# Computing the first four chunks of a squared-relu projection whole, and starting the half-size products with the fifth

## The chip, the cores and the metric

The kernel runs on one core of a Trainium2 chip. The metric is device time in microseconds (us), the median of several executions. Five engines work side by side and meet through semaphores: TensorE (PE; its weight loads are listed as PEld), VectorE (DVE), ScalarE (ACT), GpSimd (POOL) and SyncE (SP, which here only issues DMAs).

## The reference, cut to what matters

Two transformer-like blocks follow one another over 512 positions and 1024 channels, each with two layers, all in float32. The change touches the last part of each layer of the second block:

```python
h = rms_norm(x, g_ffn[l])
x = x + jnp.square(jax.nn.relu(h @ w_ff1[l])) @ w_ff2[l]      # w_ff1: 1024 x 4096
```

Just before it comes `x = x + merged @ w_out[l]`.

## The kernel before, in words

Everything is kept transposed: a tile holds 128 channels by 512 positions. Float32 products are made from rounded parts: a value is split into a high part (ScalarE copies it to the rounded type) and a low part (VectorE subtracts; `split`, lines 126 and 127), and one product is three matmuls, high by high, high by low, low by high (`mm3`, lines 153 to 155). A `gemm` loads one 128-column chunk of weights (512 KB, one DMA), splits it, and runs 8 x 3 = 24 matmuls of 128x512 into one PSUM bank.

The first projection of the squared relu (`w_ff1_2`) has 32 chunks in each layer. The kernel takes them in pairs, 16 `Unit`s, and computes each pair with Strassen's scheme in Winograd's form: the pair is a 2x2 block product (two chunks by two halves of the channels by two halves of the positions), done with seven products of half the positions in place of eight. Each of the seven products is 4 x 3 = 12 matmuls of 128x256 (`product`, lines 194 to 196), so a unit has 84 of them; the same pair through `gemm` would be 48 matmuls of 128x512. The scheme needs sums of both operands. Of the weights, GpSimd forms four 128x512 sums per unit (lines 214 to 217), and they, too, are split. Of the moving operand, `moving_parts` forms for each pair of channel tiles two tiles of differences (lines 168 to 171, tiles `d`) and splits both, the second tile of the pair and the first half of the first tile (tiles `hah`, `hal` for that half, `hh`, `hl` for the rest). That is done once per layer, while the eight chunks of the output projection `w_out_2` are computed (loop at line 996): chunk m gives `x[m]` (line 998), then its square for the norm, then the scaled copy `hf` (line 1001); after every second chunk the pair's parts are made. Every unit needs the parts of all four pairs.

The norm's factor is not applied to the operand. It is a vector over positions that commutes with relu, so it is squared and applied after the second projection (line 1049). Its chain: GpSimd and VectorE add up the squares (tiles `sqa`), TensorE sums them over channels (`ss`, line 271), VectorE takes the inverse square root in some 15 tiny operations (lines 277 to 295) and multiplies it into an identity matrix (`dh`, `dl`), and TensorE spreads it over the partitions (`sp`, lines 302 and 303). In the program this stands between the first unit's products 1, 2, 5 (`one`) and its products 6, 3 (`two`). After every fourth unit a quarter of the second projection (`w_ff2_2`) runs, 8 `gemm`s.

The order of instructions on each engine is not the program's. A planner sorts them at build time by the program's order as priority and by its own prices for each instruction: what is ready in its plan goes ahead of what isn't. At run time each engine keeps to that fixed order. Buffers in rotation: 4 raw weight tiles, 4 high and 4 low weight tiles, 2 tiles for the sums of the weights, 32 tiles `hl` for split operands, 8 `work` tiles, PSUM banks in tags of 3 (`mm`), 2 (`t`), 2 (`sc`) and 1 (`o`).

Of the kernel before, what the change touches and what calls it, by code (L numbers as in the profile page):

```python
# [10 lines left out]
F32R = mybir.dt.float32r  # L11
I32 = mybir.dt.int32
AF = mybir.ActivationFunctionType
ALU = mybir.AluOpType
# [4 lines left out]
HS = S // 2  # L19
D = 1024  # L20
KD = D // P
# [37 lines left out]
def two_blocks(ctx: ExitStack, tc: tile.TileContext, g: dict):  # L59
    nc = tc.nc  # L60
    V, A, G, T = nc.vector, nc.scalar, nc.gpsimd, nc.tensor
# [8 lines left out]
    def uniq(n):  # L70
        cnt[0] += 1
        return f"{n}_{cnt[0]}"

    def work(n="w", shape=(P, S), dt=F32):
        return ap_.tile(list(shape), dt, tag="work", name=uniq(n), bufs=WORK)

    def gate(n="g", shape=(P, S), dt=F32):
        return ap_.tile(list(shape), dt, tag="gate", name=uniq(n), bufs=16)

    def hl(n="hl", dt=F32R):  # L80
        return ap_.tile([P, S], dt, tag="hl", name=uniq(n), bufs=32)
# [4 lines left out]
    def mmps(n="mm"):  # L86
        return ps.tile([P, S], F32, tag="mm", name=uniq(n), bufs=3)
# [10 lines left out]
    def ops(n="o"):  # L98
        return ps.tile([P, S], F32, tag="o", name=uniq(n), bufs=1)


    x = [ap_.tile([P, S], F32, tag=f"x{k}", name=f"x{k}", bufs=1) for k in range(KD)]
# [4 lines left out]
    def col(name, l, c):  # L107
        o, w = VCOL[name]
        o += l * w + c
        return vec[:, o : o + 1]  # L110
# [12 lines left out]
    def split(src, hi, lo, scale=None, n=None):  # L123

        if scale is None:
            A.activation(hi, src, AF.Copy)  # L126
            V.tensor_tensor(lo, src, hi.bitcast(F32), op=ALU.subtract)  # L127
        else:
            A.activation(hi, src, AF.Copy, scale=scale)
            V.scalar_tensor_tensor(lo, src, scale, hi.bitcast(F32), op0=ALU.mult, op1=ALU.subtract)  # L130

    def split_tile(src, scale=None, n="h"):
        hi, lo = hl(n + "h"), hl(n + "l")
        split(src, hi, lo, scale)
        return hi, lo

    def weights(dram, kk, m):

        n = kk * m
        raw = wp.tile([P, CH], F32, tag="raw", name=uniq("raw"), bufs=RAW)  # L140
        nc.sync.dma_start(out=raw[:, :n], in_=dram)
        hi = wp.tile([P, CH], F32R, tag="whi", name=uniq("whi"), bufs=WBUF)
        lo = wp.tile([P, CH], F32R, tag="wlo", name=uniq("wlo"), bufs=WBUF)
        split(raw[:, :n], hi[:, :n], lo[:, :n])
        h = hi[:, :n].rearrange("p (k m) -> p k m", k=kk)
        l = lo[:, :n].rearrange("p (k m) -> p k m", k=kk)
        return h, l

    def mm3(out, terms, first=True, last=True):

        n = len(terms)
        for i, ((wh, wl), (xh, xl)) in enumerate(terms):
            T.matmul(out, lhsT=wh, rhs=xh, start=(first and i == 0), stop=False)  # L153
            T.matmul(out, lhsT=wh, rhs=xl, start=False, stop=False)  # L154
            T.matmul(out, lhsT=wl, rhs=xh, start=False, stop=(last and i == n - 1))  # L155

    def gemm(dram, xs, order=None):

        kk = len(xs)
        h, l = weights(dram, kk, P)  # L160
        out = mmps()
        mm3(out, [((h[:, k, :], l[:, k, :]), xs[k]) for k in order or range(kk)])
        return out

    def moving_parts(b1, b2, odd, o):

        d1, d2 = work("d1"), work("d2")
        V.tensor_tensor(d1[:, :HS], b1[:, HS:], b1[:, :HS], op=ALU.subtract)
        V.tensor_tensor(d1[:, HS:], b2[:, HS:], d1[:, :HS], op=ALU.subtract)
        V.tensor_tensor(d2[:, :HS], b2[:, HS:], b1[:, HS:], op=ALU.subtract)  # L170
        V.tensor_tensor(d2[:, HS:], b2[:, :HS], d1[:, HS:], op=ALU.subtract)
        split(b1[:, :HS], odd[0][:, o : o + HS], odd[1][:, o : o + HS])
        out = [tuple(t[:, o : o + HS] for t in odd)]
        for t in (b2, d1, d2):
            pair = split_tile(t, None, "h")
            out += [tuple(p[:, :HS] for p in pair), tuple(p[:, HS:] for p in pair)]
        return dict(zip((1, 2, 3, 5, 6, 7, 4), out))

# [96 lines left out]
    def mean_eps(ss, n):  # L275
        v = small("v")[:, : ss.shape[1]]
        V.tensor_scalar(v, ss, 1.0 / n, EPS, op0=ALU.mult, op1=ALU.add)
        return v

    def rsqrt(v):  # L280

        y, t = small("y")[:, : v.shape[1]], small("t")[:, : v.shape[1]]
        V.tensor_scalar(y.bitcast(I32), v.bitcast(I32), 1, None, op0=ALU.arith_shift_right)
        V.tensor_scalar(y.bitcast(I32), y.bitcast(I32), -1.0, float(0x5F3759DF), op0=ALU.mult, op1=ALU.add)
        for _ in range(3):
            V.tensor_tensor(t, y, y, op=ALU.mult)
            V.scalar_tensor_tensor(t, t, -0.5, v, op0=ALU.mult, op1=ALU.mult)
            V.scalar_tensor_tensor(y, t, 1.5, y, op0=ALU.add, op1=ALU.mult)
        return y
# [142 lines left out]
    def scaled(p, R, n="e", alloc=work):  # L432
        t = alloc(n)
        V.tensor_tensor(t, p, R, op=ALU.mult)  # L434
        return t
# [5 lines left out]
    p = ops("idle")  # L441
# [11 lines left out]
    for j in range(KD + len(FIRST) - 1):  # L453
        for i, c in enumerate(FIRST):
            k = j - i
            if 0 <= k < KD:
                h, lo = first_w[c]
                mm3(first[c], [((h[:, k, :], lo[:, k, :]), xs[k])], k == 0, k == KD - 1)
    ident = const("ident", (P, P))
    sq = SumSq(V)  # L460
# [12 lines left out]
    for c in (CK, CV):  # L473
        first[c] = scps()
        h, lo = weights(g["w_in"][0, c], KD, P)
# [26 lines left out]
    for l in range(DEPTH):  # L502
        def proj(c):
            return first.pop(c) if c in first else gemm(g["w_in"][l, c], xs)
# [72 lines left out]
        for c in range(2):  # L577
            t, r = ts[c], work("cqr")
            rope(t, cos, sin, r, acopy)
            cq.append(queries(r, hl, "cqx"))  # L580
        t = scaled(proj(CK), R, "ck")
# [12 lines left out]
        for c in range(2):  # L594
            v = scaled(proj(AV + c), R, "av")
            t = work("avt")
            A.activation(t, v, AF.Tanh, scale=0.5)
            u = scaled(proj(AU + c), R, "au")
# [134 lines left out]
        sq = SumSq()  # L733
# [3 lines left out]
        for m in range(KD):  # L737
            p = gemm(g["w_out"][l, m], y, (4, 5, 2, 6, 7, 3, 0, 1))
# [30 lines left out]
    o, w = VCOL["lru_lambda_2"]  # L769
# [21 lines left out]
    for l in range(DEPTH):  # L791
# [13 lines left out]
        for c in range(2):  # L805
            t = scaled(proj(5 + c), R, "kl")
# [4 lines left out]
        for c in range(3):  # L811
            t = scaled(proj(2 + c), R, "ql")
# [164 lines left out]
        for m in range(KD):  # L977
            tg = {0: gate_of(0, m, work), 2: gate_of(2, m, work), 1: tg1[m]}
            h, lo = weights(g["w_br"][l, m], 8, P)
            acc = None  # L980
            for i, k0, ops_ in ((0, 0, ypool), (2, 6, ylru), (1, 2, yo)):
                p = mmps("br")
                mm3(p, [((h[:, k0 + k, :], lo[:, k0 + k, :]), ops_[k]) for k in range(len(ops_))])
                t = work("mgt")
# [7 lines left out]
            mg.append((hi, lo))  # L992

        sq = SumSq()
        hs, halves, odd = [], [], None
        for m in range(KD):
            p = gemm(g["w_out_2"][l, m], mg)
            V.scalar_tensor_tensor(x[m], p, 0.5, x[m], op0=ALU.mult, op1=ALU.add)
            sq.add(x[m])
            t = work("hf")  # L1000
            A.activation(t, x[m], AF.Copy, scale=col("g_ffn_2", l, m))
            halves.append(t)
            if m % 2:
                if m % 4 == 1:
                    odd = hl("hah"), hl("hal")
                hs.append(moving_parts(halves[m - 1], t, odd, m // 2 % 2 * HS))

        sums = sq
        sq = SumSq()
        nxs = []  # L1010
        last = l == DEPTH - 1
        units = [Unit(g["w_ff1_2"][l, 2 * u], g["w_ff1_2"][l, 2 * u + 1], hs) for u in range(16)]

        def relu2(t, n):
# [6 lines left out]
            split(t, hi, lo)  # L1021
            return hi, lo

        f = {}
        for u in range(17):
            if u < 16:
                units[u].one()
            if u == 0:
                rf = rsqrt(mean_eps(token_sums(sums.parts()), D))
                V.tensor_tensor(rf, rf, rf, op=ALU.mult)  # L1030
                Rf2 = spread(rf)
            if u:
                units[u - 1].three()
            if u < 16:
                units[u].two()
            if u:
                units[u - 1].four()
                f[2 * u - 1] = relu2(units[u - 1].bottom, 1)
            if u % 4 or not u:
                f[2 * u] = relu2(units[u].top, 0)  # L1040
                continue
            qt = u // 4 - 1
            fq = [f[8 * qt + c] for c in range(8)]
            if last and qt == 3:
                break
            for m in range(KD):
                p = gemm(g["w_ff2_2"][l, qt, m], fq)
                t = work("ff")
                V.tensor_tensor(t, p, Rf2, op=ALU.mult)  # L1049
                V.tensor_tensor(x[m], x[m], t, op=ALU.add)  # L1050
                if qt == 3:
                    sq.add(x[m])
                    nxs.append(split_tile(x[m], col("g_mix_2", l + 1, m), "x"))
            if u < 16:
                f[2 * u] = relu2(units[u].top, 0)
# [7 lines left out]
    for h in range(2):  # L1063
        t = ap_.tile([P, S + 64], F32, tag="pad", name=uniq("gf"), bufs=3)[:, :S]
# [4 lines left out]
    for h in range(2):  # L1069
# [5 lines left out]
        for b in range(4):  # L1075
# [6 lines left out]
            p = mmps("last")  # L1082
            mm3(p, [((fq[k][0][:, ts], fq[k][1][:, ts]), ws[k]) for k in range(KD)])
            if h == 0 and b % 2 == 0:
                pair = ap_.tile([P, 10 * P], F32, tag="prob", name=uniq("yh"), bufs=PROBS)
            yh = pair[:, S * (b % 2) : S * (b % 2) + S] if h == 0 else xt
            V.scalar_tensor_tensor(yh, p, rf[:, b : b + 1], xt, op0=ALU.mult, op1=ALU.add)
            sq = work("sq")
# [122 lines left out]
```

## Time and profile before

| | |
|---|---|
| median of 3 runs | 1929.95 us (1928.28 to 1930.03) |
| profiled execution, its own time | 1930.22 us |
| its span, first to last instruction | 1928.3 us, mean granted TensorE clock 0.992 |
| PE busy | 1872.7 us (97%), 10028 matmuls |
| DVE busy | 1376.5 us (71%) |
| ACT busy | 933.0 us (48%) |
| POOL busy | 274.9 us (14%) |

Matmuls overlap in the pipeline, so the duration of one is longer than the distance from one start to the next; what a matmul costs is read from that distance. "Idle before" is the time that an engine stood still before an instruction, and the arrow names what it then waited for.

### The profile page before, as it was taken

What the parts mean: (1) busy time and instruction counts of PE and PEld (TensorE: products, weight loads), DVE (VectorE), ACT (ScalarE), POOL (GpSimd) and SP (SyncE); (2) the same over time, 40 slices, a digit from 0 to 9 for tenths busy, and PEclk for the clock granted to TensorE, in tenths of its full rate; (3) what the DMA queues carried; (4) which work ended last, traced back from release to release, by engine and by line L of the source; (5) the groups of instructions that cost most, each with busy time, mean ns of one, the idle gap of its engine ahead of it and who ended that gap; (6) DMA issues with size and microseconds to landing.
All of it is one profiled execution on the core that took longest, in us unless ns stands there. A gap on an engine that the chain in (4) does not pass through costs nothing.

```text
span 1928.3 us, 26111 instructions
## 1 busy us (share of the span) xinstructions
PE 1872.7 (97%) x10028; PEld 1565.1 (81%) x10028; DVE 1376.5 (71%) x2304; ACT 933.0 (48%) x1567; POOL 274.9 (14%) x211
## 2 busy tenths in 40 slices
PE   9999999999989999998999999999999989999998
PEld 7877878878857788878898998777788879889896
DVE  8997669976788545588576777687455687667584
ACT  7565445654358533265253444367433455344362
POOL 0000100002100000043133141000000132424121
PEclk9999999999989999999999999999999999999999
DMA  6322323222212223221322323222232313232321
GB/s 216 107 80 82 98 88 96 77 77 90 64 44 95 71 87 98 99 88 66 109 99 88 110 88 120 62 85 87 66 98 92 105 44 113 88 107 94 125 88 44
DMA packets 53693, 175.41 MB, mean 91 GB/s; under 512 B 6208, under 2 KB 10176, under 8 KB 53568
## 3 DMA queue, kind: packets, MB, share of 16 engines
q1 hardware_dynamic: 53568, 173.74, 27.8%
q8 instruction: 79, 1.29, 0.3%
q14 instruction: 46, 0.38, 0.1%
HBM read 171.62 MB, written 2.10 MB: 90 GB/s over the span
## 4 chain that ended last, share of the span: by engine, by line
PE 79%; DVE 12%; issue 4%; ACT 4%; DVEq 0%; ACTq 0%
PE mm L154 17%; PE mm L153 17%; PE mm L155 17%; DVE ul L127 2%; PE o L417 2%; PE ua L194 2%; PE t L337 2%; PE ua L196 2%; PE ua L195 2%; PE sc L860 2%; PE br L153 2%; PE br L154 2%; PE br L155 2%; DVE fl L127 1%; PE sc L553 1%
## 5 line engine op out<-in xcount | busy, mean ns | idle before, releaser
L126 ACT ACTIVATE whi<-raw 128x1024 fp32r<-128x1024 f32 (+2 forms) x250 | 252.1, 1012 | 529.4 <-PE mm L154 388.6
L153 PE MATMUL mm<-xh,whi 128*128 128x512 f32 x904 | 361.7, 401 | 0.4 <-DVE ql L434 0.4
L155 PE MATMUL mm<-xh,wlo 128*128 128x512 f32 x904 | 357.6, 396 | 0.0
L154 PE MATMUL mm<-xl,whi 128*128 128x512 f32 x904 | 356.8, 395 | 0.0
L127 DVE TENSOR_TENSOR wlo<-raw,whi 128x1024 fp32r<-128x1024 f32 (+2 forms) x250 | 300.6, 1205 | 36.6 <-ACT whi L126 35.0
L153 PEld LDWEIGHTS mm<-xh,whi 128*128 128x128 f32 x904 | 170.5, 189 | 37.7 <-issue 3.8
L155 PEld LDWEIGHTS mm<-xh,wlo 128*128 128x128 f32 x904 | 170.4, 189 | 36.5 <-issue 2.2
L154 PEld LDWEIGHTS mm<-xl,whi 128*128 128x128 f32 x904 | 170.6, 189 | 35.3 <-issue 2.7
L153 PE MATMUL mm<-fh,whi 128*128 128x512 f32 x448 | 174.4, 389 | 0.0
L154 PE MATMUL mm<-fl,whi 128*128 128x512 f32 x448 | 174.4, 389 | 0.0
L155 PE MATMUL mm<-fh,wlo 128*128 128x512 f32 x448 | 174.3, 389 | 0.0
L214 POOL TENSOR_TENSOR s<-raw 128x512 f32<-128x512 f32 x32 | 48.3, 1510 | 833.9 <-DVE hl L127 461.3
L1049 DVE TENSOR_TENSOR ff<-mm,rstd 128x512 f32<-128x512 f32 x56 | 38.7, 691 | 119.8 <-PE mm L155 119.6
L434 DVE TENSOR_TENSOR lg<-mm,rstd 128x512 f32<-128x512 f32 x48 | 33.2, 691 | 119.6 <-PE mm L155 119.5
L194 PE MATMUL ua<-hh,uh 128*128 128x256 f32 x384 | 110.5, 288 | 6.6 <-DVE bottom L248 5.7
L195 PE MATMUL ua<-hl,uh 128*128 128x256 f32 x384 | 109.1, 284 | 0.0
L196 PE MATMUL ua<-hh,ul 128*128 128x256 f32 x384 | 109.0, 284 | 0.0
L155 PEld LDWEIGHTS mm<-fh,wlo 128*128 128x128 f32 x448 | 84.1, 188 | 17.6
L153 PEld LDWEIGHTS mm<-fh,whi 128*128 128x128 f32 x448 | 84.1, 188 | 17.2
L154 PEld LDWEIGHTS mm<-fl,whi 128*128 128x128 f32 x448 | 84.1, 188 | 17.1
L126 ACT ACTIVATE uh<-s 128x1024 fp32r<-128x1024 f32 x64 | 67.5, 1059 | 60.9 <-PE mm L154 26.6
L127 DVE TENSOR_TENSOR ul<-s,uh 128x1024 fp32r<-128x1024 f32 x64 | 87.0, 1377 | 6.0 <-ACT uh L126 6.0
(366 smaller groups left out, 4319.0 us busy)
## 6 DMA issues: line engine op xcount, KB each, us to landing
raw<-in_w_in SPq DMA_DIRECT2D x124, 512.0 KB, 3.5
raw<-in_w_ff SPq DMA_DIRECT2D x120, 512.0 KB, 3.3
raw<-in_w_out SPq DMA_DIRECT2D x32, 512.0 KB, 3.4
raw<-in_w_br SPq DMA_DIRECT2D x16, 512.0 KB, 3.3
raw<-in_w_last SPq DMA_DIRECT2D x8, 512.0 KB, 4.0
raw<-in_w_q SPq DMA_DIRECT2D x12, 192.0 KB, 2.3
x<-in_xT SPq DMA_DIRECT2D x8, 256.0 KB, 5.8
bends<-in_rpb SPq DMA_DIRECT2D x8, 256.0 KB, 4.7
```

Of the source, the lines that this page charges most:

```text
L126: A.activation(hi, src, AF.Copy)
L127: V.tensor_tensor(lo, src, hi.bitcast(F32), op=ALU.subtract)
L153: T.matmul(out, lhsT=wh, rhs=xh, start=(first and i == 0), stop=False)
L154: T.matmul(out, lhsT=wh, rhs=xl, start=False, stop=False)
L155: T.matmul(out, lhsT=wl, rhs=xh, start=False, stop=(last and i == n - 1))
L194: T.matmul(out, lhsT=h[:, ks], rhs=xh, start=(first and j == 0), stop=False, skip_group_check=True)
L195: T.matmul(out, lhsT=h[:, ks], rhs=xl, start=False, stop=False, skip_group_check=True)
L196: T.matmul(out, lhsT=lo[:, ks], rhs=xh, start=False, stop=(last and j == 3), skip_group_check=True)
L214: G.tensor_tensor(s1[:, :S], a21, a22, op=ALU.add)
L337: T.matmul(out, lhsT=in_, rhs=ident, is_transpose=True, start=True, stop=True)
L417: T.matmul(out[64 * j : 64 * j + 64, i * P : (i + 1) * P], lhsT=v(b), rhs=t[:, at[j, e]], start=(b == keys[i][0]), stop=(b == keys[i][1] - 1))
L1049: V.tensor_tensor(t, p, Rf2, op=ALU.mult)
```

## The change

The first two units of each layer are dropped. Their four chunks are computed by `gemm` from whole split tiles, with relu on ScalarE, the square on VectorE, and a split. To have whole tiles, every scaled tile `t` is now split over all 512 positions as soon as it is there (`whole`), and `moving_parts` takes its halves from these splits. The parts of the last pair are made after the first two of the four chunks. The sum of squares comes after the split. The norm's factor now stands behind the first products of the third unit (u = 2), which is the first one left.

```diff
-    def moving_parts(b1, b2, odd, o):
+    def moving_parts(b1, b2, p1, p2):
         d1, d2 = work("d1"), work("d2")
 ...
-        split(b1[:, :HS], odd[0][:, o : o + HS], odd[1][:, o : o + HS])
-        out = [tuple(t[:, o : o + HS] for t in odd)]
-        for t in (b2, d1, d2):
-            pair = split_tile(t, None, "h")
+        out = [tuple(p[:, :HS] for p in p1)]
+        for pair in (p2, split_tile(d1, None, "h"), split_tile(d2, None, "h")):
             out += [tuple(p[:, :HS] for p in pair), tuple(p[:, HS:] for p in pair)]
 ...
         for m in range(KD):
             p = gemm(g["w_out_2"][l, m], mg)
             V.scalar_tensor_tensor(x[m], p, 0.5, x[m], op0=ALU.mult, op1=ALU.add)
-            sq.add(x[m])
             t = work("hf")
             A.activation(t, x[m], AF.Copy, scale=col("g_ffn_2", l, m))
             halves.append(t)
-            if m % 2:
-                if m % 4 == 1:
-                    odd = hl("hah"), hl("hal")
-                hs.append(moving_parts(halves[m - 1], t, odd, m // 2 % 2 * HS))
+            whole.append(split_tile(t, None, "h"))
+            sq.add(x[m])
+            if m % 2 and m < KD - 1:
+                hs.append(moving_parts(halves[m - 1], t, *whole[m - 1 : m + 1]))
 ...
+        f = {}
+
+        def plain(u):
+            for c in (2 * u, 2 * u + 1):
+                p = gemm(g["w_ff1_2"][l, c], [whole[k] for k in (0, 2, 4, 6, 1, 3, 5, 7)])
+                t = work("relu")
+                A.activation(t, p, AF.Relu)
+                V.tensor_tensor(t, t, t, op=ALU.mult)
+                f[c] = gate("fh", dt=F32R), gate("fl", dt=F32R)
+                split(t, *f[c])
+
+        plain(0)
+        hs.append(moving_parts(*halves[KD - 2 :], *whole[KD - 2 :]))
+        plain(1)
 ...
-        for u in range(17):
+        for u in range(2, 17):
             if u < 16:
                 units[u].one()
-            if u == 0:
+            if u == 2:
                 rf = rsqrt(mean_eps(token_sums(sums.parts()), D))
                 V.tensor_tensor(rf, rf, rf, op=ALU.mult)
                 Rf2 = spread(rf)
-            if u:
+            if u > 2:
                 units[u - 1].three()
             if u < 16:
                 units[u].two()
-            if u:
+            if u > 2:
                 units[u - 1].four()
                 f[2 * u - 1] = relu2(units[u - 1].bottom, 1)
-            if u % 4 or not u:
+            if u % 4:
                 f[2 * u] = relu2(units[u].top, 0)
                 continue
```

## Rows read from the trace of the kernel before

**Rows 1.** TensorE's waits, 813 to 1190 us: us in total, times, longest.
```profile
PE sp L302 <- DVE dh L299: 4.1, 1, 4.1
PE ua L194 <- DVE bottom L248: 2.8, 4, 0.8
PE ss L271 <- DVE sqa L333: 1.0, 1, 1.0
PE ub L195 <- DVE hl L127: 0.8, 1, 0.8
```
**Rows 2.** Timeline of TensorE: start us, us, engine, line, operation [idle before, releaser].
```profile
813.46 0.39 PE L153 MATMUL mm<-mh,whi 128*128 128x512 f32 x1
...
856.98 0.28 PE L194 MATMUL ua<-hah,uh 128*128 128x256 f32 x1
...
870.01 1.02 PE L271 MATMUL ss<-ones,sqa 128*128 128x1 f32 x8 [1.04 <-DVE sqa L333]
870.89 0.37 PE L194 MATMUL ua<-hah,uh 128*128 128x256 f32 x1
...
873.37 0.28 PE L196 MATMUL uc<-hh,ul 128*128 128x256 f32 x1
877.75 0.80 PE L302 MATMUL sp<-dh,ones_r 128*128 128x512 f32 x1 [4.10 <-DVE dh L299]
...
881.11 0.28 PE L194 MATMUL ua<-hh,uh 128*128 128x256 f32 x1
...
886.86 0.28 PE L194 MATMUL ua<-hah,uh 128*128 128x256 f32 x1
...
1560.79 0.28 PE L194 MATMUL ua<-hah,uh 128*128 128x256 f32 x1
...
1573.84 1.02 PE L271 MATMUL ss<-ones,sqa 128*128 128x1 f32 x8 [1.04 <-DVE sqa L333]
...
1581.58 0.79 PE L302 MATMUL sp<-dh,ones_r 128*128 128x512 f32 x1 [4.09 <-DVE dh L299]
...
1589.01 0.28 PE L194 MATMUL uc<-hh,uh 128*128 128x256 f32 x1
```
**Rows 3.** Stretches: length, busy time by engine, granted clock, DMA share, GB/s.
```profile
877.75:880.69 2.94, 2.94 (x11) 2.75 (x12) 1.06 (x5) 1.24 (x3) 0.00 (x0) 0.50 0.00 0
1581.58:1587.29 5.71, 5.71 (x24) 5.52 (x25) 1.49 (x6) 3.48 (x6) 0.00 (x0) 0.50 0.00 0
```
**Rows 4.** Timeline of TensorE, the same chain of a norm among full-size matmuls.
```profile
266.06 0.95 PE L271 MATMUL ss<-ones,sqa 128*128 128x1 f32 x8
...
271.65 0.50 PE L302 MATMUL sp<-dh,ones_r 128*128 128x512 f32 x1 [0.17 <-DVE dh L299]
```
**Rows 5.** Timeline of VectorE.
```profile
267.92 1.23 DVE L127 TENSOR_TENSOR wlo<-raw,whi 128x1024 fp32r<-128x1024 f32 x1
...
850.04 1.51 DVE L170 TENSOR_TENSOR d<-hf,hf 128x256 f32<-128x256 f32 x1
...
856.33 0.69 DVE L998 SCALAR_TENSOR_TENSOR x<-mm,x 128x512 f32<-128x512 f32 x1
...
863.41 0.41 DVE L170 TENSOR_TENSOR d<-hf,hf 128x256 f32<-128x256 f32 x1
...
864.09 0.68 DVE L127 TENSOR_TENSOR hl<-hf,hh 128x512 fp32r<-128x512 f32 x1
...
871.99 0.15 DVE L277 TENSOR_SCALAR v<-ss 128x4 f32<-128x4 f32 x1
...
872.38 1.15 DVE L284 TENSOR_SCALAR y<-y 128x4 int32<-128x4 int32 x1
873.56 1.18 DVE L286 TENSOR_TENSOR t<-y 128x4 f32<-128x4 f32 x1
...
875.17 0.16 DVE L286 TENSOR_TENSOR t<-y 128x4 f32<-128x4 f32 x1
```
**Rows 6.** Tile `s` alone, one stretch: DVE, ACT, POOL busy, clock, DMA.
```profile
857.00:878.00 21.00, 4.66 (x3) 2.12 (x2) 8.41 (x6) 0.99 0.15 51
```
**Rows 7.** Timeline of GpSimd.
```profile
872.21 1.29 POOL L216 TENSOR_TENSOR s<-raw,s 128x512 f32<-128x512 f32 x1 [1.23 <-DVE v L277]
873.46 1.26 POOL L217 TENSOR_TENSOR s<-raw,raw 128x512 f32<-128x512 f32 x1
```

More of the change, by code (lines that the diff above doesn't have):

```diff
@@ L994, in two_blocks @@
         sq = SumSq()
-        hs, halves, odd = [], [], None
+        hs, halves, whole = [], [], []
         for m in range(KD):
@@ L1022, in relu2 @@
             return hi, lo
-        f = {}
-        for u in range(17):
+        for u in range(2, 17):
             if u < 16:
                 units[u].one()
-            if u == 0:
+            if u == 2:
                 rf = rsqrt(mean_eps(token_sums(sums.parts()), D))
```

## The prediction

> **What bounds the kernel now.** I read the page first: TensorE is busy for 97% of the span, so a change counts only through what TensorE executes and where it stands still. The view of waits says where it stands still: in the second block's squared relu it waits at the start of each layer, once for long on the spreading of the norm's factor (`sp`, 4.1 us) and several times for under 1.1 us on `sqa`, `hl` and its kin, while all later units together show four waits of at most 0.8 us on `bottom` [rows 1]. Last I read TensorE's timeline, for the distances from start to start.
>
> Full-size matmuls: from 813.46 to 856.98 run the 8 x 24 = 192 of the output projection, 43.52 / 192 = 0.2267 us each. Half-size ones: from 881.11 to 886.86 run four products of 12, 5.75 / 48 = 0.12 us each [rows 2]. So the scheme pays 53% per half-size matmul, and a unit's 84 cost 10.08 us.
>
> What the start of a layer loses: from 856.98 to 870.01 there are 63 half-size matmuls (five products of 12 and three of the next unit), 7.56 us of work in 13.03 us; 5.47 us are lost while the last pair's parts and the sum of squares come late. The second layer has the same 13.05 us from 1560.79 [rows 2]. The parts come late because VectorE is behind: TensorE is done with chunk 6 at 856.98 - 24 x 0.2267 = 851.5, yet `x[6]` is only computed at 856.33, behind the third pair's subtractions, of which one took 1.51 us where the same one takes 0.41 elsewhere [rows 5].
>
> Then the norm: behind `ss` stand 21 half-size matmuls, the last at 873.37, and `sp` starts at 877.75: 877.75 - 873.49 = 4.26 us of standing still [rows 2]. The granted clock behind it is 0.50 (1.2 GHz) for 2.9 us in the first layer and 5.7 us in the second [rows 3]; from `sp` to 881.11 there are 12 half-size matmuls and two full ones, 1.89 us of work in 3.36; in the second layer, from 1581.58 to 1589.01, 36 and two, 4.77 in 7.43 [rows 2]. So the slow clock costs 1.5 and 2.7 us, and the norm's wait with it 2 x 4.26 + 1.5 + 2.7 = 12.7 us in two layers.
>
> **The change part by part.** *More matmul work.* Four units of 10.08 us become four pairs of chunks of 48 x 0.2267 = 10.88 us: 4 x 0.80 = +3.2 us, all on the path, since TensorE has nothing else.
>
> *The waits at the start go.* The first chunk takes its operands in the order 0, 2, 4, 6, 1, 3, 5, 7, so it needs tile 6 after 9 matmuls, 2.0 us in (859.0 on the old time axis), and tile 7 after 21, 4.8 us in (861.7). Chunk 7 of the output projection ends with TensorE at 857.0; then one update (0.69), the scaled copy and high part on ScalarE, the low part (0.68) [rows 5], with the hand-overs some 3.5 us: 860.5, 1.2 us early. Tile 6 has 5.4 us more and can bear most of the lateness that it has now. The last pair's differences, which stand in the way now, come after the first two chunks. The chunks' weights are four DMAs of 512 KB in place of the same four; a raw tile is given back after one split instead of after GpSimd's four sums, so nothing behind them on SP's queue is later. I count 0.3 us per layer as left over (bounds 0, by the 1.2 us of slack, and 5.5, by the loss now): gain 2 x (5.5 - 0.3) = 10.4 us. The wait for `sqa` is in this sum; with 22 us of full-size chunks behind it, it can't come last again.
>
> *Wider splits and other relus.* Tiles 0, 2, 4, 6 are split over 512 instead of 256 positions, the four chunks are squared on VectorE (nearest row 0.68), while eight GpSimd sums a layer and the splits of two units fall away. Cover: TensorE's 21.8 us of whole chunks. VectorE's work in that stretch, unstretched: update 0.69, two weight splits 2.5, the last tile's low part 0.68, the last pair 4 x 0.41 + 2 x 0.68 = 3.0, `sqa` 0.7, four squares and four low parts 5.4, the third unit's weights 4.3, the start of the fourth's 1.9: 19.2 us [rows 5]. It fits, at 88%. If it does not, the third unit is late (the last rival).
>
> *The norm's factor moves* behind the third unit's first three products. What matters is what the planner puts between `ss` and `sp`. Among full-size matmuls the chain took 271.65 - 266.06 = 5.59 us, and the planner had filled it to within 0.17 us [rows 4], which is 4.4 us or some 20 matmuls of 0.2267. Among half-size ones it put 21 [rows 2], which take 2.5 us. It counts a half-size matmul like a full one, so its plan falls short by 5.59 - 0.88 (`ss`) - 2.52 = 2.2 us even with a chain that runs freely. The other 2 us of today's 4.26 are two tiny operations of the chain that took 1.15 and 1.18 us instead of 0.16 [rows 5], at the very times of two GpSimd sums [rows 7]. In the plan TensorE has ready work of higher priority until the third unit's three products are issued, so I expect `ss` right behind them and `sp` behind the 24 matmuls of `two`: half-size ones again. Bounds for the wait: 0.3 (the row among full-size matmuls) and 4.3 (today's). I take the middle of 2.2 and 4.3, since GpSimd is busy beside the units for a part of the time: 3.2 us, and the smaller of the two prices of the slow clock, 1.5: 4.7 per layer, 9.4 in two. Gain 12.7 - 9.4 = 3.3 us.
>
> The collision has a rule. The Trainium skill, GPSIMD Engine Reference, section Specifications, says that GpSimd's SBUF interfaces are shared with VectorE and that they contend with VectorE's instructions of two SBUF inputs or in a two-port mode; the subtraction of 1.51 us against 0.41 agrees. By the rule alone every such operation beside a GpSimd sum is late; what that would make of the whole chunks is the last rival.
>
> *Sum.* 1930.2 (the profiled execution, 1928.3 of span and 1.9 around it) + 3.2 - 10.4 - 3.3 = 1919.7. That execution stands 0.3 us above the median of the runs, so I predict 1919.5.
>
> **The rivals.**
>
> A, the forecast: 1919.5. With a free chain and no slow clock (2 x 2.2 left of 12.7, no rest at the start): 1930.2 + 3.2 - 10.9 - 8.3 = 1914.2. With 1 us left at each start and the norm's wait as it is: 1930.2 + 3.2 - 8.9 = 1924.5. Chance 0.53.
>
> B, the norm's wait goes too: the planner finds a gap earlier and puts `ss` and `sp` among the whole chunks, where its price for a matmul holds. For it: the squares are summed 15 us before the third unit starts, and the row among full-size matmuls. Against it: the order in the program, and no gap in sight. 0.3 us left per layer and no slow clock: 1930.2 + 3.2 - 10.4 - 12.1 = 1910.9. Chance 0.23.
>
> C, the first chunks wait instead: `x[6]` and tile 7 stay behind the third pair's parts on VectorE, as `x[6]` does now by 4.8 us. For it: the splits in front of them are wider. Against it: the third and fourth units' sums start later. Half of the loss comes back (2.7 per layer), the norm's wait stays: 1930.2 + 3.2 - 5.5 = 1927.9, no measurable change. So the change would do what it says and gain nothing. Chance 0.14.
>
> D, slower: VectorE does not get through the whole chunks. GpSimd's sums took 8.4 us in the 21 us after 857 [rows 6]; if the third and fourth units' sums fall into the same stretch and hold up VectorE by all of it, 19.2 + 8.4 = 27.6 us stand against 21.8, the last pair's parts and the third unit's weights, lowest in priority, are 5.8 us late, and the norm's wait stays: 1930.2 + 3.2 - 10.9 + 11.6 = 1934.1. It decides where the last pair's splits end after the fourth chunk. This is the rule of the Trainium skill (GPSIMD Engine Reference, Specifications) taken in full. Against it: in the rows not every operation beside a sum is stretched, and the planner can put parts earlier. Chance 0.10.
>
> **How the numbers follow.** About 0.2% (3.9 us) can be told from no change, so faster means under 1926.1. A gives nearly all of its 0.53, B 0.23, C some 0.03: 0.79. The same: most of C and a little of A, 0.12. Slower: 0.09, from D. The range from 1909 to 1927 takes in B with 2 us to spare and A whole, some 0.8; C and D lie outside. A's own range is 1914 to 1924.5.
>
> **What would show it.** Right: no TensorE wait over 0.5 us in the four whole chunks, whose 96 matmuls take 21.8 us; one wait of 2 to 4.3 us on `dh` per layer, behind some 20 to 24 half-size matmuls, with a clock of 0.50 behind it; units as before from the fourth on. Wrong: `sp` among 128x512 matmuls (B); waits on `hl` inside the first chunk (C); waits on `hl` or `ul` at the third unit's first product (D).

## The result, and the profile after

The changed kernel takes 1919.93 us (median, 1919.07 to 1921.59) against 1929.99 us of the kernel before beside it: ratio 0.9949, 95% interval 0.9932 to 0.9966. That is 10 us or 0.5% faster; 1919.5 was forecast, with a range of 1909 to 1927. The profiled execution took 1920.23 us with a span of 1918.3 us, 10.0 us less than before. The total came out as forecast, and in part by luck: one of its terms was wrong by 4.4 us, and a gain of 3.6 us that was not counted made up for it.

TensorE's waits between 813 and 1190 us, the stretch of [rows 1] (us in total, times, longest):

```profile
PE sp L300 <- DVE dh L297: 3.8, 1, 3.8
PE ua L192 <- DVE bottom L246: 1.5, 2, 0.8
PE ss L269 <- DVE sqa L331: 0.7, 1, 0.7
```

The waits on `hl` and its kin at the start of a layer are gone. The wait on `dh` is as good as unchanged, the one on `sqa` is still there, and of four waits on `bottom` two are left.

TensorE's timeline after, in both layers (start, us, engine, line, operation): first matmul of the output projection, first half-size one, `ss`, `sp`, the first matmul behind the stretch at the slow clock, first one of the second projection (`ss` and `sp` in the first layer only).

```profile
814.20 0.39 PE L153 MATMUL mm<-mh,whi 128*128 128x512 f32 x1
...
879.82 0.28 PE L192 MATMUL ua<-hh,uh 128*128 128x256 f32 x1
...
886.88 1.02 PE L269 MATMUL ss<-ones,sqa 128*128 128x1 f32 x8 [0.68 <-DVE sqa L331]
...
895.67 0.50 PE L300 MATMUL sp<-dh,ones_r 128*128 128x512 f32 x1 [3.83 <-DVE dh L297]
...
902.04 0.28 PE L192 MATMUL uc<-hh,uh 128*128 128x256 f32 x1
...
915.00 0.40 PE L153 MATMUL mm<-fh,whi 128*128 128x512 f32 x1
...
1513.41 0.39 PE L153 MATMUL mm<-mh,whi 128*128 128x512 f32 x1
...
1578.74 0.28 PE L192 MATMUL ua<-hh,uh 128*128 128x256 f32 x1
...
1601.92 0.28 PE L192 MATMUL uc<-hh,uh 128*128 128x256 f32 x1
...
1614.88 0.40 PE L153 MATMUL mm<-fh,whi 128*128 128x512 f32 x1
```

The ends of the same stretch in the kernel before, where its first row is the first of [rows 2]:

```profile
918.88 0.40 PE L153 MATMUL mm<-fh,whi 128*128 128x512 f32 x1
...
1517.27 0.39 PE L153 MATMUL mm<-mh,whi 128*128 128x512 f32 x1
...
1623.93 0.40 PE L153 MATMUL mm<-fh,whi 128*128 128x512 f32 x1
```

From the first matmul of the output projection to the first of the second projection the kernel before takes 918.88 - 813.46 = 105.4 us and 106.7 us, the changed one 100.8 and 101.5: 4.6 and 5.2 us less, 9.8 of the 10.0. The rest differs by less than 1 us in any stretch (0.7 more ahead of the first layer's stretch, 0.95 less behind the second's). With 0.2267 and 0.12 us per matmul, and some 1.35 for `ss` and `sp`, the work in this stretch is 192 full and 396 half-size matmuls before (92.4 us) and 288 and 228 after (94.0). By this count the price of 1.6 us per layer is there as forecast. What is lost to standing still and to the slow clock falls from 13.0 and 14.3 us to 6.8 and 7.5.

| lost, us, both layers | before | after |
|---|---|---|
| start, to the first half-size matmul after the whole chunks (before: to `ss`) | 11.0 | 0.4 |
| the norm: `ss` to the end of the slow clock (after: with the wait on `sqa`) | 12.8 | 13.9 |
| from there to the second projection (two waits on `bottom` per layer, with what stands about them) | 3.6 | 0 |

In the view of waits those on `bottom` of the first quarter, the products ahead of the first part of the second projection, are 0.45 and 0.82 us in each layer; from start to start of the matmuls they cost 1.8.

### The profile page after: what moved, and what is told of

Same layout as the page of the kernel before. It is cut to its first block, busy times and chain, and to the rows that moved or that the text cites. A ratio compares the mean times of both kernels' runs of the same rounds, so it can differ in the third digit from the quotient of the medians.

```text
span 1918.3 us, 25753 instructions
## 1 busy us (share of the span) xinstructions
PE 1872.8 (98%) x9884; PEld 1560.5 (81%) x9884; DVE 1353.7 (71%) x2288; ACT 922.5 (48%) x1543; POOL 248.3 (13%) x195
## 4 chain that ended last, share of the span: by engine, by line
PE 82%; DVE 10%; ACT 4%; issue 4%; DMA 0%; SPq 0%; DVEq 0%; ACTq 0%
PE mm L154 18%; PE mm L153 18%; PE mm L155 18%; PE o L415 2%; PE t L335 2%; DVE ul L127 2%; PE ua L192 2%; PE ua L194 2%; PE ua L193 2%; PE sc L858 2%; PE br L153 2%; PE br L154 2%; PE br L155 2%; PE sc L551 1%; DVE wlo L127 1%
## 5 line engine op out<-in xcount | busy, mean ns | idle before, releaser
L126 ACT ACTIVATE whi<-raw 128x1024 fp32r<-128x1024 f32 (+2 forms) x258 | 260.6, 1014 | 537.5 <-PE mm L154 389.8
L127 DVE TENSOR_TENSOR wlo<-raw,whi 128x1024 fp32r<-128x1024 f32 (+2 forms) x258 | 315.4, 1225 | 39.0 <-ACT whi L126 37.7
L192 PE MATMUL ua<-hh,uh 128*128 128x256 f32 x448 | 128.3, 286 | 3.4 <-DVE bottom L246 3.4
L193 PE MATMUL ua<-hl,uh 128*128 128x256 f32 x448 | 127.6, 285 | 0.0
L194 PE MATMUL ua<-hh,ul 128*128 128x256 f32 x448 | 127.6, 285 | 0.0
L323 POOL TENSOR_TENSOR sqa<-sq,sq 128x512 f32<-128x512 f32 x8 | 12.0, 1503 | 629.7 <-DVE d L170 456.1
L212 POOL TENSOR_TENSOR s<-raw 128x512 f32<-128x512 f32 x28 | 42.5, 1517 | 381.7 <-DMA raw<-in_w_ff 216.9
L192 PEld LDWEIGHTS ua<-hh,uh 128*128 128x128 f32 x448 | 87.0, 194 | 5.1 <-DVE bottom L246 4.8
```

The lines of the kernel that those rows point to most:

```text
L192: T.matmul(out, lhsT=h[:, ks], rhs=xh, start=(first and j == 0), stop=False, skip_group_check=True)
L193: T.matmul(out, lhsT=h[:, ks], rhs=xl, start=False, stop=False, skip_group_check=True)
L194: T.matmul(out, lhsT=lo[:, ks], rhs=xh, start=False, stop=(last and j == 3), skip_group_check=True)
L212: G.tensor_tensor(s1[:, :S], a21, a22, op=ALU.add)
```

## The experiments

Two start from the kernel before (the order of the splits alone, and the second of the two with the later spreading), the others from the changed kernel. Each was timed in turn with the kernel before on the same chip; the medians of the kernel before, 1929.8 to 1930.0 us, agree.

**The norm's chain among the whole chunks.**

```diff
         plain(0)
+        rf = rsqrt(mean_eps(token_sums(sums.parts()), D))
+        V.tensor_tensor(rf, rf, rf, op=ALU.mult)
+        Rf2 = spread(rf)
         hs.append(moving_parts(*halves[KD - 2 :], *whole[KD - 2 :]))
 ...
-            if u == 2:
-                rf = rsqrt(mean_eps(token_sums(sums.parts()), D))
-                V.tensor_tensor(rf, rf, rf, op=ALU.mult)
-                Rf2 = spread(rf)
```

> The chain of the norm's factor is moved up, to between the second and the third whole chunk; 24 full-size matmuls then stand between ss and sp, where 32 half-size ones stood. Theory (the planner counts half-size matmuls as full ones, so the chain is covered only among full ones): the wait on dh falls from 3.8 us to 0.5 or less in each layer, no clock of 0.50 behind it, the wait on sqa goes; of the 13.9 us that the norm costs in two layers some 12.5 go: 1907.5 us. Rival (VectorE is the bound of the whole chunks, 88% full by my count, and the chain's 5 us push the third unit's weights and the last pair's parts late): waits on ul or hl at the third unit of 2 to 3 us per layer, 1913 to 1919 us.

1912.45 us, ratio 0.9912 (0.9898 to 0.9925): 7.5 us below the changed kernel, between the two expectations. `sp` still waits, and VectorE's and GpSimd's timelines of this run show for what:

```profile
872.18 1.25 DVE L281 TENSOR_SCALAR y<-v 128x4 int32<-128x4 int32 x1
873.47 0.17 DVE L282 TENSOR_SCALAR y<-y 128x4 int32<-128x4 int32 x1
873.67 1.13 DVE L284 TENSOR_TENSOR t<-y 128x4 f32<-128x4 f32 x1
```
```profile
871.79 1.61 POOL L212 TENSOR_TENSOR s<-raw 128x512 f32<-128x512 f32 x1 [8.93 <-issue]
873.48 1.30 POOL L213 TENSOR_TENSOR s<-s,raw 128x512 f32<-128x512 f32 x1
```
```profile
PE sp L300 <- DVE dh L297: 2.0, 1, 2.0
```

Two tiny operations take 1.25 and 1.13 us where they take 0.17 and 0.16 alone, 2.05 us too long, beside two of GpSimd's sums; the one between them, which was under way when the second sum began, took 0.17. The wait is 2.0 us. Among full-size matmuls the plan covers the chain, but not what GpSimd adds to it. No unit waits on `ul` or `hl`, so it is not the rival's mechanism: two waits of 2.0 us and the slow clock behind one of them (1.5 us) are about what is missing to 1907.5.

**Only two whole chunks.**

```diff
         hs.append(moving_parts(*halves[KD - 2 :], *whole[KD - 2 :]))
-        plain(1)
 ...
-        for u in range(2, 17):
+        for u in range(1, 17):
```

(and u = 1 in place of u = 2 in the conditions)

> Only the first two chunks of each layer are whole, the half-size products begin with the third chunk. Theory (two chunks are too short a cover for the last pair's parts, and a run of three units brings back the wait on bottom): 1.6 us less of matmul work, 1 us per layer of waits on d or hl at the first unit, 1 us per layer on bottom: 1919.9 - 1.6 + 4 = 1922 us. Rival (the start waits are covered by any whole chunk, and a whole pair costs just its 0.8 us): 1918.3 us.

1927.45 us, ratio 0.9987 (0.9978 to 0.9996): 7.5 us worse than with four chunks, and 5 worse than I expected.

```profile
PE sp L300 <- DVE dh L297: 5.5, 1, 5.5
PE ua L192 <- DVE bottom L246: 2.0, 3, 0.8
PE mm L154 <- DVE hl L127: 1.6, 2, 0.9
```

The wait comes back at the start, but on `hl` inside the whole chunks, not at the first unit; and the one on `dh` grows to 5.5, with a weight split of 2.19 us and three operations of the chain at 1.25, 1.10 and 1.19 us, beside four sums from 879.61 to 885.7. One wait on `bottom` in the first quarter, 0.45 us, is back as well, on the third of its three units. So the start loses 2.4 us per layer (240 full matmuls in 56.84 us) where I had expected 1, and the chain's part, 1.7 us more per layer on `dh`, stood in neither expectation.

**The order of the splits alone, in the kernel before.**

```diff
             V.scalar_tensor_tensor(x[m], p, 0.5, x[m], op0=ALU.mult, op1=ALU.add)
-            sq.add(x[m])
 ...
                 hs.append(moving_parts(halves[m - 1], t, odd, m // 2 % 2 * HS))
+            sq.add(x[m])
```

> The kernel before, with one part of the change alone: the sum of squares comes behind the splits and the differences instead of ahead of them; no chunk is whole. Theory (the start waits come from half-size products that want the last pair at once): within 1 us of before, 1929 to 1930.5 us, with the four waits at the layer's start in place. Rival (the order of the splits made the gain): 1921 to 1925 us, and the four waits shorter by half or more.

1930.92 us, ratio 1.0005 (0.9996 to 1.0014): no change. In the first layer the wait on `sqa` is gone and the two on the last tile (`ub`) fall from 1.5 to 0.2 us, the two on `hah` and `hal` grow, and the wait on `dh` takes the rest back:

```profile
PE sp L302 <- DVE dh L299: 5.3, 1, 5.3
PE ua L194 <- ACT hah L126: 0.9, 1, 0.9
PE ua L195 <- DVE hal L127: 0.9, 1, 0.9
```

At the start 4.7 us are lost per layer in place of 5.5 (54 half-size matmuls in 11.2 us). So the order alone does not give the gain at the start; and what is saved ahead of the norm's chain can be lost in it.

**No sums of GpSimd beside the chain.**

```diff
+            if self.sums:
                 s1 = ap_.tile(...)
 ...
                 G.tensor_tensor(s2[:, S:], a11, a21, op=ALU.subtract)
+            else:
+                s1, s2 = raws
 ...
+        units = [Unit(g["w_ff1_2"][l, 2 * u], g["w_ff1_2"][l, 2 * u + 1], hs, u != 4) for u in range(16)]
```

> The changed kernel with GpSimd's four sums left out for the fifth unit of each layer (u = 4), the one whose sums fall into the norm's chain; the raw weights are split in their place, so the fifth unit's products are not the reference's. TensorE's order stays the same. Theory (collision of GpSimd's sums with VectorE's tiny operations): the chain gets 3.0 us shorter, the wait on dh falls from 3.8 to about 0.9 us, the clock stays at 1.00, and 2 x (3.0 + 1.5 to 2.7) are gained: 1910 us. Rival (the planner's price alone makes the wait): the wait stays at 2.2 us or more, 1915 to 1919 us.

1909.22 us, ratio 0.9895 (0.9881 to 0.9908), 10.7 us below the changed kernel, as the theory had it. VectorE's timeline of the changed kernel, then GpSimd's, then this run's VectorE (its lines stand three further down) and its wait:

```profile
887.95 0.16 DVE L275 TENSOR_SCALAR v<-ss 128x4 f32<-128x4 f32 x1 [1.21 <-PE ss L269]
888.14 1.11 DVE L281 TENSOR_SCALAR y<-v 128x4 int32<-128x4 int32 x1
...
890.89 1.15 DVE L286 SCALAR_TENSOR_TENSOR y<-t,y 128x4 f32<-128x4 f32 x1
892.07 1.19 DVE L284 TENSOR_TENSOR t<-y 128x4 f32<-128x4 f32 x1
```
```profile
887.94 1.29 POOL L213 TENSOR_TENSOR s<-s,raw 128x512 f32<-128x512 f32 x1
890.73 1.29 POOL L214 TENSOR_TENSOR s<-raw,s 128x512 f32<-128x512 f32 x1 [1.50 <-DVE t L284]
891.97 1.26 POOL L215 TENSOR_TENSOR s<-raw,raw 128x512 f32<-128x512 f32 x1
```
```profile
888.42 0.17 DVE L284 TENSOR_SCALAR y<-v 128x4 int32<-128x4 int32 x1
...
890.22 0.16 DVE L289 SCALAR_TENSOR_TENSOR y<-t,y 128x4 f32<-128x4 f32 x1
890.42 0.16 DVE L287 TENSOR_TENSOR t<-y 128x4 f32<-128x4 f32 x1
```
```profile
PE sp L303 <- DVE dh L300: 0.9, 1, 0.9
```

Each of the three operations starts within 0.2 us of a sum and ends where the sum ends. Without the sums they take 0.16 to 0.17, 2.96 us less in all, and the wait falls by 2.94, from 3.83 to 0.89 us. The slow clock goes with it: the granted clock stays at 1.00 behind `sp` in both layers. What is left, 0.9 us, is what the planner's order leaves uncovered. The Trainium skill, GPSIMD Engine Reference, section Specifications, names the contention for SBUF interfaces with VectorE's operations of two SBUF inputs or in a two-port mode. The trace agrees for L286 and L284, which have two inputs, and adds the size: the VectorE operation is held to the end of the sum. L281 has one input and was held as well; in which mode it runs, no run shows.

Not every VectorE operation is held. In the changed kernel, VectorE's timeline and then GpSimd's:

```profile
857.14 1.78 DVE L127 TENSOR_TENSOR hl<-hf,hh 128x512 fp32r<-128x512 f32 x1
858.85 0.68 DVE L996 SCALAR_TENSOR_TENSOR x<-mm,x 128x512 f32<-128x512 f32 x1
```
```profile
856.64 1.74 POOL L213 TENSOR_TENSOR s<-s,raw 128x512 f32<-128x512 f32 x1
858.45 1.62 POOL L214 TENSOR_TENSOR s<-raw,s 128x512 f32<-128x512 f32 x1
```

The split of `hf` is held (0.68 alone, [rows 5]); the update behind it, which reads its product `mm` from PSUM, runs inside a sum at its usual 0.68. In the traces of the ten kernels, around the two layers' squared relu, 61 single operations that read a product from PSUM began inside a GpSimd operation (its last 0.1 us left out), and none took over 0.15 us more than its shortest; of 379 without such an input 370 did.

**The spreading one unit later, and the same in the kernel before.**

```diff
-                Rf2 = spread(rf)
 ...
                 units[u].two()
+            if u == 3:
+                Rf2 = spread(rf)
```

(in the kernel before: `if u == 1`)

> The changed kernel, with only the spreading of the norm's factor moved down by one unit (behind the products 6, 3 of the fourth unit); ss and the inverse square root stay. Between ss and sp stand 83 half-size matmuls (10 us) instead of 32. Theory (the wait is the chain's length less the work put beside it, so enough work beside it removes it and the slow clock behind it): no wait on dh, clock 1.00, 2 x 4.0 + 1.5 + 2.7 us gained: 1907.7 us. Rival (VectorE is late anyway, and the standing still let it catch up): waits on bottom or ul of the later units take back half: 1913 us or more.

1910.96 us, ratio 0.9904 (0.9889 to 0.9919): 9 of the 12.2 us. The chain met three sums here too (1.12, 1.14 and 1.22 us), but under 83 matmuls. Some wait is left, 1.4 us, and for another reason. The factor was there at 892.7 (L292 at 892.69 is the first rounding), but the multiplications into the identity had slid behind the units' splits in VectorE's queue:

```profile
892.69 0.17 DVE L292 CAST yh<-y 128x4 fp32r<-128x4 f32 x1
...
893.91 1.22 DVE L127 TENSOR_TENSOR ul<-raw,uh 128x1024 fp32r<-128x1024 f32 x1
895.05 0.42 DVE L246 TENSOR_TENSOR bottom<-ua,keep 128x256 f32<-128x256 f32 x1
895.38 1.22 DVE L127 TENSOR_TENSOR ul<-s,uh 128x1024 fp32r<-128x1024 f32 x1
896.51 0.87 DVE L297 TENSOR_SCALAR dh<-c_ident,yh 128x128 fp32r<-128x128 f32 x4
```
```profile
PE sp L300 <- DVE dh L297: 1.4, 1, 1.4
```

The rival's place (`bottom`) shows hardly more than in the changed kernel, 3.8 us in both layers against 3.4.

> The kernel before, no chunk whole, with only the spreading moved down by one unit in the same way (72 half-size matmuls between ss and sp instead of 21). Theory (the norm's wait and the waits at the start are separate losses): the start's waits stay (5.5 us per layer), the wait of 4.26 us and the slow clock go: 1929.9 - 2 x 4.26 - 4.2 = 1917.2 us. Rival (as above, half comes back on bottom): 1923 us.

1919.56 us (1919.22 to 1923.79), ratio 0.9954 (0.9941 to 0.9966), between the expectations: one moved line in the kernel before gives as much as the whole change. The profiled execution was the longest, 1923.79 us. In it the waits at the start stay as in [rows 1], as expected; the waits on `dh` are 1.1 us in one layer and 2.6 in the other. Here the multiplication into the identity itself is held beside a sum:

```profile
882.56 1.88 DVE L299 TENSOR_SCALAR dh<-c_ident,yh 128x128 fp32r<-128x128 f32 x4
```

The same four together took 0.87 us in the run above. The slow clock did not go as expected: in the first layer it came between `ss` and `sp`, behind the waits at the start, and in the second behind the 2.6 us. The two waits on `bottom` in the first quarter are gone too, though all four of its units are there.

**Six whole chunks, without and with the later spreading.**

```diff
         plain(1)
+        plain(2)
 ...
-        for u in range(2, 17):
+        for u in range(3, 17):
```

(and u = 3 in place of u = 2; with the later spreading also `if u == 4` behind `two`)

> The changed kernel with six whole chunks instead of four, half-size products from the seventh on. Theory (a further pair costs its 0.8 us and hides nothing more, since the start's waits are gone with four): 1919.9 + 1.6 = 1921.5 us, the wait on dh within 0.5 us of 3.8. Rival (each unit less relieves VectorE, and the norm's chain runs freely): the wait falls below 2 us, 1914 us.

1910.21 us, ratio 0.9899 (0.9886 to 0.9913): 9.7 us below four chunks, where I expected 1.6 above. GpSimd's timeline, the stretch of the chain (length, busy times of PE, PEld, DVE, ACT and POOL, clock, DMA) and TensorE's wait:

```profile
887.92 1.74 POOL L215 TENSOR_TENSOR s<-raw,raw 128x512 f32<-128x512 f32 x1
```
```profile
897.00:901.60 4.60, 3.76 (x32) 3.56 (x30) 4.15 (x21) 0.38 (x1) 0.00 (x0) 1.00 0.00 0
```
```profile
PE sp L300 <- DVE dh L297: 0.9, 1, 0.9
```

The order between `ss` and `sp` is the same 32 half-size matmuls. But GpSimd's last sum ends at 889.7, the chain runs from 896.9 to 901.5 with GpSimd idle (the fifth column of busy times, 0.00), since behind the fifth unit the weights of the second projection come in line before those of the sixth: GpSimd's next sum begins at 932.2. The wait is 0.89 us, to the hundredth the one without sums. The price of a pair is there: by the same count as above the stretch holds 94.8 us of work, and 96.3 are spent.

> Six whole chunks and the spreading one unit later together. Theory: as the four chunks with the later spreading, plus the price of a pair in each layer: 1.6 us above that run, about 1909.3 us. Rival (VectorE's relief counts): the same as that run or below.

1908.29 us, ratio 0.9887 (0.9874 to 0.9901), the fastest version: 11.6 us below the change, and 1.9 us below six chunks alone. No wait is left but the 0.8 us on `bottom` in later quarters:

```profile
PE ua L192 <- DVE bottom L246: 1.6, 2, 0.8
```

It is not slower than four chunks with the later spreading (1910.96), as the price alone would have made it, because those still waited 1.4 us on `dh` and 0.7 on `sqa` per layer: 1.6 - 2.8 - 1.4 = -2.6, measured -2.7.

## Why the prediction was right, point by point

**The price of whole chunks**, +3.2 us: held. The work in the stretch grew by 1.6 us per layer, by the count of its matmuls.

**The waits at the start**, -10.4: held, 11.0 - 0.4 = 10.6 us. With two whole chunks 1.6 us of waits stand there again in the first layer, and the order alone saves nothing in total. Part of the same step failed: the wait on `sqa` was to go for good, and is 0.7 us per layer as it moved. The squares' last addition stood in VectorE's order behind weight splits of the fourth unit, at 886.05 us, some 28 us after the last chunk of the output projection.

**The norm's wait**, -3.3: failed. Forecast were 9.4 us left of 12.7; measured are 13.9 with the wait on `sqa` (0.8 per layer with its hand-over), so some 12.2 without it: nearly nothing gained (per layer 4.0 us of standing still, and 1.6 and 2.6 us of slow clock where I took the smaller price for both). The step had two parts. That the planner's order would leave the chain uncovered among half-size matmuls was right, but mis-sized: 0.9 us per layer, not 2.2, with 32 matmuls between `ss` and `sp` in place of the 24 I counted on. My chain of 5.59 us [rows 4] also had a weight split of 1.23 in it [rows 5]. Without sums beside it, and with such a split in it, the wait is 0.9 us in two kernels. The collision with GpSimd was to be halved and was the larger part: 3.0 us per layer after, 2.0 before. Before, the chain also started 1.1 us after `ss` ended, behind a split that stood beside a sum of 869.39 to 870.98 (1.22 us elsewhere):

```profile
869.78 2.28 DVE L127 TENSOR_TENSOR ul<-s,uh 128x1024 fp32r<-128x1024 f32 x1
```

So about 3 us of the 4.26 were GpSimd's before as well, and only some 1.2 the plan's, not 2.2. That the planner counts a half-size matmul like a full one, on which the 2.2 rested, is not shown: it put 32 half-size ones into this chain and 24 full-size ones into that of the first experiment.

**What I had not counted**: 3.6 us with the waits on `bottom` in the first quarter went. So +3.2 - 10.6 + 1.1 - 3.6 = -9.9, where the two stretches lost 9.8 us. A run of more than two units is not enough for the waits on `bottom`, since they also went in the kernel before once the norm's wait was shorter; nor is the norm's wait, which the changed kernel still has, with two units in the first quarter and no such wait. With three units and a wait of 5.5 us there was one of 0.45. That VectorE is late behind the norm's wait and gets later with each unit fits this, and was not tried by itself. **Rivals**: B (the chain moves among the whole chunks by itself), C and D did not come about. D's mechanism is real, and it fell on the whole chunks too (the split of 1.78 us at 857.14), but TensorE did not wait there; what it cost, it cost in the chain. The sum was thus right by luck: +4.4 us at the norm and -3.6 on `bottom` nearly cancelled.

## What to carry to other kernels

A chain of many tiny operations on VectorE is lengthened by sums that GpSimd forms at that time, here by about 1 us for each sum of 1.3 us in which one of its operations begins (those that read PSUM aside): place such a chain where GpSimd is idle, or put enough work between its ends, before paying for anything else. Where a planner fixes the order, read from the trace what it put between the two ends of a chain and how long that takes; what it covers in its own prices is not what is covered on the chip. A small edit far from the critical wait (one pair of chunks more) can move another engine's work off it, so a price computed from matmul counts alone can have the wrong sign.

## What the runs showed of the hardware that I had not expected

One operation of 128x4 elements, 0.16 us alone, takes 1.10 to 1.25 us beside a GpSimd sum of 128x512, and it does not matter whether it has one input or two: L281 (one input, a scalar) took 1.11 us and L284 (two inputs) 1.19. And the same wait of 1.97 us left TensorE at 1.2 GHz in one layer and at 2.4 in the other, in the run with the chain among the whole chunks (stretches behind `sp`; granted clock is the column behind the busy times):

```profile
877.91:881.25 3.34, 3.34 (x8) 2.66 (x9) 3.34 (x10) 1.26 (x3) 0.00 (x0) 0.50 0.00 0
1574.32:1577.60 3.28, 3.28 (x14) 2.61 (x15) 3.28 (x10) 2.04 (x4) 0.00 (x0) 1.00 0.00 0
```

In the runs with waits of 1.1 and 1.4 us on `dh` no slow clock followed. But no single long wait is needed for it either. In the kernel before with the later spreading, five waits of 0.7 to 1.1 us at the start of the first layer, the last at `ss` (872.21), were followed by this stretch, while `sp` came only at 884.58:

```profile
874.62:877.83 3.21, 3.21 (x17) 3.21 (x16) 3.00 (x8) 2.61 (x5) 2.32 (x2) 0.50 0.00 0
```

So the wait that stands just ahead of a slow stretch need not be its only cause.
